# A two-layer trunk with attention: the norms' inverse roots reach all partitions by a round trip through device memory (softmax heads) and by transposes of a repeated column (the other norms)

## The chip, the cores and the metric

The kernel runs on one core of a Trainium2 chip. The metric is the device time of one execution in microseconds; for the kernel before, three runs gave 1161.12, 1161.31 and 1162.6, a median of 1161.31 us. The engines of the core are named as in the profile: PE (matrix products), DVE, ACT and POOL (elementwise work), and SP, whose queue issues most of the transfers. Each engine executes its own program in order; semaphores tie the programs together.

## The reference

The input is (1, 512, 1024) in float32: 512 tokens of 1024 features. Each of two layers normalizes x, projects it to 3072 columns, runs eight stick-breaking heads of 64 features (a sigmoid in place of a softmax) and four differential heads (two softmaxes each, subtracted), normalizes every differential head by its 128 features, projects back, and adds a squared-ReLU network of 4096. One more norm ends it. The parts that the change touches:

```python
def rmsnorm(x, g):
    xf = x.astype(jnp.float32)
    y = xf * lax.rsqrt(jnp.mean(xf * xf, axis=-1, keepdims=True) + EPS) * g.astype(jnp.float32)
...
def differential_attention(q, k, v, lam):
...
        p = jax.nn.softmax(jnp.where(allowed, s, neg), axis=-1)
        attn = p[:, :, 0] - lam * p[:, :, 1]
        return jnp.einsum('bhqk,bhkd->bhqd', attn.astype(vh.dtype), vh)
...
        h = rmsnorm(x, attn_norm[l])
        proj = jnp.einsum('bsd,de->bse', h, w_in[l])
...
        df_out = (rmsnorm(df_heads, subln_norm[l]) * (1.0 - lambda_init)).reshape(B, S, DF_WIDTH)
        mixed = jnp.concatenate([sb_out, df_out.astype(sb_out.dtype)], axis=-1)
        x = x + jnp.einsum('bse,ed->bsd', mixed, w_o[l])
        h = rmsnorm(x, mlp_norm[l])
        u = jnp.square(jax.nn.relu(jnp.einsum('bsd,df->bsf', h, w_ff1[l])))
        x = x + jnp.einsum('bsf,fd->bsd', u, w_ff2[l])
    return rmsnorm(x, final_norm)
```

Every one of these norms multiplies each token by one number, the inverse root of a mean of squares.

## The kernel before, in words

**Layout.** Activations stand with the features on the 128 partitions and the 512 tokens along the row. A norm's factor, one number for each token, is therefore needed as a row of 512 numbers that is the same on all 128 partitions. All large products are made of three matmuls (`three`, L278): every operand is split into a high and a low part, and high by high, high by low and low by high are summed (L281 to L283 by the trace). `split` (L223) makes the parts: the high one on ACT (L224), the low one on DVE (L225).

**A norm, first half: `rms_a` (L244).** PE transposes the squares in four blocks of 128 tokens (L248), so that tokens stand on partitions; DVE sums along the row (L249) and scales the mean (L251, or L253 with a floor of its own for each token); POOL raises it to the power of minus one half (L259). The result is a column: 128 partitions by 4 blocks, `rcol` for the attention norm (a) and the MLP norm (m), `rc` for a differential head (d). Then DVE splits the column into `chi` and `clo` (L260, L261), and four 128 by 128 diagonal matrices of each are made (L264, L266), on DVE for a and m, on POOL for d.

**Second half: `rms_b` (L271).** PE multiplies a matrix of ones by the two diagonals (L274, L275), which puts each token's factor into a row on every partition, and ACT copies that from PSUM (L276), to `rbc` for a and m and to a tile `rb` of its own for d.

**The attention stage of a layer.** `dense` (L710) runs the input projection block by block in a fixed order: d0, w0, d1, w1, d2, w2, d3, w3, s0, u0, s1, u1, s2, u2, s3, u3, then the output projection of the differential heads (`wo`, L691). d is a differential head's queries and keys, w its values; s and u are the same of a pair of stick-breaking heads. Projections that come before the norm's factor is known are held back and evicted when a step counter reaches RB (32 in the first layer, 31 in the second); there `rms_b` of norm a stands, with the multiplication of the rotation tables `cos_t` and `sin_t` by `rbc`. `rms_a` stands at step RA (21 and 20). Evicted d heads are rotated (`evict_d`, L442): u and v by `cos_t` and `sin_t`, then, deferred by 3.5 us of a modelled clock, sums, a split into `hl`, and twelve moves by SP's queue (`move`, L420) into the stacks `st` (high parts) and `kl` (low parts) that the score matmuls read (L477 and L478).

Beside it runs the generator `attn` (L667): scores of a unit (`s1_df`, `s1_sb`), transposes of the weights two units later (`s2`), products with the values three units later (`s3`). The loop at L744 mixes the two: every yielded step of the projection advances a modelled clock by the cost of its matmuls and gives attention a credit; attention's steps spend it, each by the cost that it yields. A unit is let in when the clock has passed a due time set at its eviction (6 us for s, 8 us for d). `defer` (L407) runs a function when the clock has passed.

When a differential head is complete, `start_norm` (L638) calls `rms_a` with the head's squares, and one unit later `finish` (L646) calls `rms_b`, lets POOL multiply the head's output `os` by `rb` (L650), and splits it into `mdh` and `mdl` (L651), which only the output projection reads. Both yield a cost of 0.43 to the clock.

**The MLP.** Groups of eight hidden blocks follow one another; norm m's `rms_a` stands at the start of the second block of the first group (L943), its `rms_b` in the third (L945); the first two blocks wait in PSUM until then.

**Order and queues.** The tile framework's scheduler orders each engine's program from the emitted one; nothing is fixed by hand. SP's queue carries the weights' raw loads, the moves and loads of tables.

Of the kernel before, what the change touches and what calls it, by code (L numbers as in the profile page):

```python
# [9 lines left out]
F32 = mybir.dt.float32  # L10
# [7 lines left out]
P = 128  # L18
S = 512
# [12 lines left out]
LAG2, LAG3, KSB = 2, 3, 7  # L32
MTB = 1
TB = 5
RST = 2
WARM = 10
RA, RB, DLY_V = (21, 20), (32, 31), 3.5
# [114 lines left out]
def trunk(ctx, tc, xT, w, w2, gains, gfin, lamv, cos, sin, out):  # L152
# [5 lines left out]

    banks = {"t": 2, "mm": 2, "s": 3, "o": 1}
# [36 lines left out]
    ones = cp.tile([P, 1], F32, tag="ones", name="ones")  # L196
    nc.vector.memset(ones, 1.0)
# [18 lines left out]
    chi = cp.tile([P, 4], F32R, tag="chi", name="chi")  # L216
    clo = cp.tile([P, 4], F32, tag="clo", name="clo")
    ones_r = cp.tile([P, 1], F32R, tag="onesr", name="ones_r")
    nc.vector.memset(ones_r.bitcast(F32), 1.0)
    fin = cp.tile([P, 24], F32, tag="fin", name="fin")  # L220
    cp.tile([P, 88], F32, tag="trail", name="trail")
# [22 lines left out]
    def rms_a(src, inv_n, col, name, eng, dgt, floor=None):  # L244
        pt = bank("t", "rs_" + name)
        if RST and eng is not nc.gpsimd or RST == 2:
            for j in range(4):
                nc.tensor.transpose(pt[:, j * P : (j + 1) * P], src[:, j * P : (j + 1) * P], ident)  # L248
            nc.vector.tensor_reduce(out=ms, in_=pt.rearrange("p (j f) -> p j f", j=4), axis=AX.X, op=ALU.add)  # L249
            if floor is None:  # L250
                nc.vector.tensor_scalar(out=ms, in0=ms, scalar1=inv_n, scalar2=EPS, op0=ALU.mult, op1=ALU.add)  # L251
            else:
                nc.vector.scalar_tensor_tensor(  # L253
                    out=ms, in0=ms, scalar=inv_n, in1=floor, op0=ALU.mult, op1=ALU.add)
        else:
            for j in range(4):
                nc.tensor.matmul(pt[:, j : j + 1], src[:, j * P : (j + 1) * P], ones, start=True, stop=True)
            nc.vector.tensor_scalar(out=ms, in0=pt[:, 0:4], scalar1=inv_n, scalar2=EPS, op0=ALU.mult, op1=ALU.add)
        nc.gpsimd.tensor_tensor(out=col, in0=ms, in1=mhalf, op=ALU.pow)  # L259
        nc.vector.tensor_copy(chi, col)  # L260
        nc.vector.tensor_sub(clo, col, chi.bitcast(F32))  # L261
        dg_hi, dg_lo = dgt("dgh" + name), dgt("dgl" + name)
        idb = ident.unsqueeze(1).to_broadcast([P, 4, P])
        eng.tensor_mul(  # L264
            dg_hi.rearrange("p (j t) -> p j t", j=4), idb, chi.bitcast(F32).unsqueeze(2).to_broadcast([P, 4, P]))
        eng.tensor_mul(  # L266
            dg_lo.rearrange("p (j t) -> p j t", j=4), idb, clo.unsqueeze(2).to_broadcast([P, 4, P]))

        return dg_hi, dg_lo

    def rms_b(bc, name, dg, tag="t"):  # L271
        dg_hi, dg_lo = dg
        pb = bank(tag, "rb_" + name)
        nc.tensor.matmul(pb, ones_r.to_broadcast([P, P]), dg_hi, start=True, stop=False)  # L274
        nc.tensor.matmul(pb, ones_r.to_broadcast([P, P]), dg_lo, start=False, stop=True)  # L275
        nc.scalar.copy(bc, pb)  # L276
# [40 lines left out]
    for l in range(L):  # L317
        with ExitStack() as actx:
# [21 lines left out]
            def tr(name):  # L340
                return a2.tile([P, S], F32R, tag="dg", name=name)

# [57 lines left out]
            dgs = {}  # L400
# [235 lines left out]
            late = []  # L636

            def start_norm():  # L638
                b, os_, sqo, rc = late[0]
                floor = a3.tile([P, 4], F32, tag="floor", name=f"floor{l}{b}")  # L640
                nc.vector.scalar_tensor_tensor(
                    out=floor, in0=tops[b], scalar=EPS, in1=tops[b], op0=ALU.mult, op1=ALU.mult)
                dgs[b] = rms_a(sqo, 1.0 / P, rc, f"d{l}{b}", nc.gpsimd, tr, floor)
                return 0.43

            def finish():  # L646
                b, os_, _, _ = late.pop(0)
                rb = tt(f"rb{l}{b}")
                rms_b(rb, f"d{l}{b}", dgs[b], "s")
                nc.gpsimd.tensor_mul(os_, os_, rb)  # L650
                split(md_hi[:, b, :], md_lo[:, b, :], os_)  # L651
                return 0.43

            def behind_scores(i, stage):
# [5 lines left out]
                if stage == 2:  # L660
                    yield finish()
# [48 lines left out]
            def dense(pts):  # L710
# [9 lines left out]
                for item in ORDER[1:]:  # L720
                    kind, b = item[0], int(item[1])
                    for which in ("qk" if kind in "ds" else "v"):
                        name = f"p{l}{kind}{b}{which}"
                        for pt in block(name, "s" if step in (16, 24, 32) else "mm"):
                            step += 1
                            if step == RA[l]:
                                dgs["a"] = rms_a(ssq, 1.0 / D, rcol, f"a{l}", nc.vector, tr)
                            if step == RB[l]:
                                rms_b(rbc, f"a{l}", dgs["a"])
# [39 lines left out]
        with ExitStack() as fctx:  # L769
# [151 lines left out]
            def diagonals():  # L921
                f = fp.tile([P, 4, S], F32R, tag="F", name=f"diag{l}")
                parts_ = iter((f[:, 0, :], f[:, 1, :]))
                return lambda name: next(parts_)

            for g in range(GROUPS):
# [13 lines left out]
                for k in range(2 * GP):  # L940
                    for n, pt in enumerate(block(f"f{l}_{g}_{k}", "any")):
                        if (g, k, n) == (0, 1, 0):
                            dg = rms_a(ssq, 1.0 / D, rcol, f"m{l}", nc.vector, diagonals())  # L943
                        if (g, k, n) == (0, 2, 4):
                            rms_b(rbc, f"m{l}", dg)  # L945
# [139 lines left out]
```

## Time and profile before

| what | value |
|---|---|
| median of three runs | 1161.31 us |
| profiled execution, its own time | 1163.8 us |
| its span | 1162.0 us |
| mean granted PE clock | 0.998 |
| POOL busy | 17% |
| ACT busy | 52% |
| bytes moved in the span | 171.67 MB |

The profile is of one execution, and its span lies inside that execution's own time. Engines are busy side by side, so shares don't add up. A wait is idle time of an engine, put down to what ended it; a matmul's record overlaps that of the next, and its cost is read from the starts. A line number is one of the kernel before; a row of the timeline gives start, duration, engine, line, operation, output from inputs, and shape. In the rows of transfers stand KB of each and the median time from issue to landing.

### The profile page before, as it was taken

The page shows a single profiled execution, that of the slowest core. Times are in us where ns is not written, and L with a number is a line of the kernel's source. Part 1 is how long each engine was busy: PE and PEld are TensorE (multiplying, and loading weights), DVE is VectorE, ACT ScalarE, POOL GpSimd, SP SyncE. Part 2 cuts the span into 40 slices and gives each one's busy share as a digit, 9 for nine tenths or more (in the row PEclk, how much of TensorE's full clock was granted, in tenths as well). Part 3 has the DMA queues.
Part 4 walks back from the last instruction along what each step waited for, and adds up shares of the span by engine and source line. Part 5 has one row for each costly group of instructions (what it writes and reads, how often), then busy time and mean ns, then how long its engine had stood idle before and what let it go on. Part 6 is the DMA issues. An engine that isn't in the chain of part 4 may idle for free.

```text
span 1162.0 us, 15297 instructions
## 1 busy us (share of the span) xinstructions
PE 1146.6 (99%) x5458; PEld 951.7 (82%) x5458; DVE 852.9 (73%) x1385; ACT 606.2 (52%) x1075; POOL 191.8 (17%) x271
## 2 busy tenths in 40 slices
PE   9999999999999999999999999999999999999996
PEld 6888888878888888888778888888888888888885
DVE  7888788777556757767888878877676577676676
ACT  6456666545645445445344566665465354453554
POOL 1011543131101001002000125332310010010021
PEclk9999999999999999999999999999999999999999
DMA  7546433146764755737526553432757557467185
GB/s 245 157 145 188 128 109 120 63 177 178 193 178 94 202 158 106 213 134 128 144 73 180 145 165 118 136 91 74 241 121 192 170 92 207 154 99 237 52 155 146
DMA packets 57291, 171.67 MB, mean 148 GB/s; under 512 B 7168, under 2 KB 8192, under 8 KB 57216
## 3 DMA queue, kind: packets, MB, share of 16 engines
q1 hardware_dynamic: 45840, 130.83, 33.9%
q0 software_dynamic: 10656, 38.80, 19.2%
q8 instruction: 43, 0.70, 0.3%
q10 hardware_dynamic: 720, 1.07, 0.2%
q14 instruction: 32, 0.26, 0.1%
HBM read 138.17 MB, written 2.10 MB: 121 GB/s over the span
## 4 chain that ended last, share of the span: by engine, by line
PE 83%; issue 5%; DMA 5%; DVE 4%; ACT 2%; POOL 1%; POOLq 0%; SPq 0%; DVEq 0%; ACTq 0%
PE f L282 9%; PE f L283 9%; PE f L281 9%; PE x L281 4%; PE x L283 4%; PE x L282 4%; PE wo L281 2%; PE wo L282 2%; DMA q<-in_w 2%; PE wo L283 2%; DMA yx<-yx 2%; DVE wlo L117 1%; PE T1s L567 1%; PE T0s L567 1%; DVE h_lo L229 1%
## 5 line engine op out<-in xcount | busy, mean ns | idle before, releaser
L282 PE MATMUL f<-h_lo,whi 128*128 128x512 f32 x512 | 199.3, 389 | 1.0 <-DVE h_lo L229 1.0
L281 PE MATMUL f<-h_hi,whi 128*128 128x512 f32 x512 | 199.7, 390 | 0.0
L116 ACT ACTIVATE whi<-raw 128x1024 fp32r<-128x1024 f32 (+1 forms) x130 | 131.9, 1019 | 129.7 <-PE f L282 40.1
L283 PE MATMUL f<-h_hi,wlo 128*128 128x512 f32 x512 | 199.3, 389 | 0.0
L116 ACT ACTIVATE whi<-q 128x512 fp32r<-128x512 f32 x224 | 128.5, 624 | 120.6 <-PE x L283 45.8
L117 DVE TENSOR_TENSOR wlo<-raw,whi 128x1024 fp32r<-128x1024 f32 (+1 forms) x130 | 153.7, 1187 | 45.1 <-ACT whi L116 44.4
L117 DVE TENSOR_TENSOR wlo<-q,whi 128x512 fp32r<-128x512 f32 x224 | 146.0, 686 | 49.2 <-ACT whi L116 49.0
L282 PEld LDWEIGHTS f<-h_lo,whi 128*128 128x128 f32 x512 | 96.1, 188 | 21.3 <-DVE h_lo L229 1.4
L283 PEld LDWEIGHTS f<-h_hi,wlo 128*128 128x128 f32 x512 | 96.1, 188 | 20.1
L281 PEld LDWEIGHTS f<-h_hi,whi 128*128 128x128 f32 x512 | 96.1, 188 | 19.7
L225 DVE TENSOR_TENSOR Al<-F,Ah 128x256 fp32r<-128x256 f32 (+2 forms) x96 | 74.4, 778 | 44.1 <-ACT Ah L224 44.1
L797 POOL DMA_DIRECT2D q<-in_w x48 | 41.9, 874 | 388.1 <-DVE wlo L117 368.2
L282 PE MATMUL x<-wlo,Ah 128*128 128x512 f32 x256 | 99.7, 390 | 0.7 <-DVE wlo L117 0.7
L281 PE MATMUL x<-whi,Ah 128*128 128x512 f32 x256 | 99.9, 390 | 0.0
L283 PE MATMUL x<-whi,Al 128*128 128x512 f32 x256 | 99.6, 389 | 0.0
L224 ACT ACTIVATE Ah<-F 128x256 fp32r<-128x256 f32 (+2 forms) x96 | 67.2, 703 | 50.4 <-DVE F L833 48.5
L824 DVE SCALAR_TENSOR_TENSOR F<-f,rbc 128x512 f32<-128x512 f32 x64 | 43.5, 687 | 64.9 <-PE f L283 57.6
L825 ACT ACTIVATE F<-F 128x512 f32<-128x512 f32 x64 | 39.7, 624 | 37.2 <-DVE F L824 37.1
L282 PEld LDWEIGHTS x<-wlo,Ah 128*128 128x128 f32 x256 | 48.1, 188 | 11.0 <-DVE wlo L117 1.1
L283 PEld LDWEIGHTS x<-whi,Al 128*128 128x128 f32 x256 | 48.0, 188 | 10.1
L281 PEld LDWEIGHTS x<-whi,Ah 128*128 128x128 f32 x256 | 48.1, 188 | 9.8
L228 ACT ACTIVATE h_hi<-x,g_all 128x512 fp32r<-128x512 f32 x32 | 22.4, 718 | 28.7 <-DVE x L704 17.5
(1055 smaller groups left out, 2556.8 us busy)
## 6 DMA issues: line engine op xcount, KB each, us to landing
raw<-in_w SPq DMA_DIRECT2D x126, 512.0 KB, 4.1
q<-in_w SPq DMA_DIRECT2D x64, 512.0 KB, 4.3
q<-in_w POOLq DMA_DIRECT2D x64, 512.0 KB, 5.4
yx<-yx POOLq DMA_DIRECT2D x6, 512.0 KB, 6.7
x<-in_xT SPq DMA_DIRECT2D x8, 256.0 KB, 4.5
raw<-in_w SPq DMA_DIRECT2D x8, 128.0 KB, 4.4
yx<-y POOLq DMA_DIRECT2D x2, 512.0 KB, 5.7
y<-y POOLq DMA_DIRECT2D x2, 512.0 KB, 8.7
```

Of the source, the lines that this page charges most:

```text
L116: h = nc.scalar.activation(hi[:, a:b], raw[:, a:b], AF.Copy)
L117: self.last = h, nc.vector.tensor_tensor(out=lo[:, a:b], in0=raw[:, a:b], in1=hi[:, a:b].bitcast(F32), op=ALU.subtract)
L224: nc.scalar.activation(hi, src, AF.Copy)
L225: nc.vector.tensor_tensor(out=lo, in0=src, in1=hi.bitcast(F32), op=ALU.subtract)
L228: a = nc.scalar.activation(h_hi[:, c, :], x[:, c, :], AF.Copy, scale=g)
L281: nc.tensor.matmul(pt, ah, bh, start=first, stop=False)
L282: nc.tensor.matmul(pt, ah, bl, start=False, stop=False)
L283: nc.tensor.matmul(pt, al, bh, start=False, stop=last)
L567: nc.tensor.transpose(pt[:, off : off + P], u["w"][qi][:, kb * P : (kb + 1) * P], ident)
L797: nc.gpsimd.dma_start(t, quad(g, q, c), accum_op=ALU.add)
L824: nc.vector.scalar_tensor_tensor(out=t, in0=pt, scalar=0.0, in1=rbc, op0=ALU.max, op1=ALU.mult)
L825: nc.scalar.activation(t, t, AF.Square)
```

## The change

The two diagonals, the matrix of ones and the column's high and low parts go. For norms a and m, `rms_b` now transposes each of the four columns of `rcol`, repeated 128 times along the row by its access pattern, which gives the row on all partitions; it stands ROW = 5 steps behind `rms_a`, and the evictions with the rotation tables stand at steps 29 and 28. For a differential head, SP's queue writes the column `rc` (128 by 4, 2 KB) to a tile in device memory, and `finish` reads it back, the same 2 KB for each of the 128 partitions (256 KB), into `rb`, in a buffer of its own. POOL's multiplication reads it in permuted order, and with the split it is deferred by 5 us of the modelled clock. `finish` costs that clock nothing. Score tiles have 8 buffers in place of 7; a pad in SBUF grows from 88 to 120 numbers; a branch that was not taken goes.

```diff
--- before.py
+++ after.py
@@ -29,12 +29,12 @@
 NEG = -1.0e30
 MMC = 0.000422
 ORDER = ("d0", "w0", "d1", "w1", "d2", "w2", "d3", "w3", "s0", "u0", "s1", "u1", "s2", "u2", "s3", "u3")
-LAG2, LAG3, KSB = 2, 3, 7
+LAG2, LAG3, KSB = 2, 3, 8
 MTB = 1
 TB = 5
-RST = 2
+ROW, DLY_N = 5, 5.0
 WARM = 10
-RA, RB, DLY_V = (21, 20), (32, 31), 3.5
+RA, RB, DLY_V = (21, 20), (29, 28), 3.5
 MAN = ()
 _CTX = {}
 DLY_R, DLY_D, DLY_S = 3.5, 8.0, 6.0
@@ -155,6 +155,8 @@
     wraw = ctx.enter_context(tc.tile_pool(name="wraw", bufs=3))
     wspl = ctx.enter_context(tc.tile_pool(name="wspl", bufs=2))
     ps = ctx.enter_context(tc.tile_pool(name="ps", bufs=2, space=PSUM))
+
+    far = ctx.enter_context(tc.tile_pool(name="far", bufs=2, space=bass.MemoryType.DRAM))
 
     banks = {"t": 2, "mm": 2, "s": 3, "o": 1}
     turn = [0]
@@ -193,8 +195,6 @@
     W.load(3)
 
     make_identity(nc, ident)
-    ones = cp.tile([P, 1], F32, tag="ones", name="ones")
-    nc.vector.memset(ones, 1.0)
     mhalf = cp.tile([P, 4], F32, tag="mhalf", name="mhalf")
     nc.vector.memset(mhalf, -0.5)
     nc.gpsimd.memset(edge[:, 0:384], 0.0)
@@ -213,12 +213,8 @@
     gsub = cp.tile([P, L], F32, tag="gsub", name="gsub")
     rcol = cp.tile([P, 4], F32, tag="rcol", name="rcol")
     ms = cp.tile([P, 4], F32, tag="ms", name="ms")
-    chi = cp.tile([P, 4], F32R, tag="chi", name="chi")
-    clo = cp.tile([P, 4], F32, tag="clo", name="clo")
-    ones_r = cp.tile([P, 1], F32R, tag="onesr", name="ones_r")
-    nc.vector.memset(ones_r.bitcast(F32), 1.0)
     fin = cp.tile([P, 24], F32, tag="fin", name="fin")
-    cp.tile([P, 88], F32, tag="trail", name="trail")
+    cp.tile([P, 120], F32, tag="trail", name="trail")
 
     def split(hi, lo, src):
         nc.scalar.activation(hi, src, AF.Copy)
@@ -241,39 +237,23 @@
         tc.add_manual_dep(a.ins, b.ins.name, mybir.DependencyInfo(
             mybir.DependencyClass.NoSync, mybir.DependencyReason.DATA), reason="order")
 
-    def rms_a(src, inv_n, col, name, eng, dgt, floor=None):
+    def rms_a(src, inv_n, col, name, floor=None):
         pt = bank("t", "rs_" + name)
-        if RST and eng is not nc.gpsimd or RST == 2:
-            for j in range(4):
-                nc.tensor.transpose(pt[:, j * P : (j + 1) * P], src[:, j * P : (j + 1) * P], ident)
-            nc.vector.tensor_reduce(out=ms, in_=pt.rearrange("p (j f) -> p j f", j=4), axis=AX.X, op=ALU.add)
-            if floor is None:
-                nc.vector.tensor_scalar(out=ms, in0=ms, scalar1=inv_n, scalar2=EPS, op0=ALU.mult, op1=ALU.add)
-            else:
-                nc.vector.scalar_tensor_tensor(
-                    out=ms, in0=ms, scalar=inv_n, in1=floor, op0=ALU.mult, op1=ALU.add)
+        for j in range(4):
+            nc.tensor.transpose(pt[:, j * P : (j + 1) * P], src[:, j * P : (j + 1) * P], ident)
+        nc.vector.tensor_reduce(out=ms, in_=pt.rearrange("p (j f) -> p j f", j=4), axis=AX.X, op=ALU.add)
+        if floor is None:
+            nc.vector.tensor_scalar(out=ms, in0=ms, scalar1=inv_n, scalar2=EPS, op0=ALU.mult, op1=ALU.add)
         else:
-            for j in range(4):
-                nc.tensor.matmul(pt[:, j : j + 1], src[:, j * P : (j + 1) * P], ones, start=True, stop=True)
-            nc.vector.tensor_scalar(out=ms, in0=pt[:, 0:4], scalar1=inv_n, scalar2=EPS, op0=ALU.mult, op1=ALU.add)
+            nc.vector.scalar_tensor_tensor(
+                out=ms, in0=ms, scalar=inv_n, in1=floor, op0=ALU.mult, op1=ALU.add)
         nc.gpsimd.tensor_tensor(out=col, in0=ms, in1=mhalf, op=ALU.pow)
-        nc.vector.tensor_copy(chi, col)
-        nc.vector.tensor_sub(clo, col, chi.bitcast(F32))
-        dg_hi, dg_lo = dgt("dgh" + name), dgt("dgl" + name)
-        idb = ident.unsqueeze(1).to_broadcast([P, 4, P])
-        eng.tensor_mul(
-            dg_hi.rearrange("p (j t) -> p j t", j=4), idb, chi.bitcast(F32).unsqueeze(2).to_broadcast([P, 4, P]))
-        eng.tensor_mul(
-            dg_lo.rearrange("p (j t) -> p j t", j=4), idb, clo.unsqueeze(2).to_broadcast([P, 4, P]))
-
-        return dg_hi, dg_lo
-
-    def rms_b(bc, name, dg, tag="t"):
-        dg_hi, dg_lo = dg
-        pb = bank(tag, "rb_" + name)
-        nc.tensor.matmul(pb, ones_r.to_broadcast([P, P]), dg_hi, start=True, stop=False)
-        nc.tensor.matmul(pb, ones_r.to_broadcast([P, P]), dg_lo, start=False, stop=True)
-        nc.scalar.copy(bc, pb)
+
+    def rms_b(bc, name, col):
+        pt = bank("t", "rb_" + name)
+        for j in range(4):
+            nc.tensor.transpose(pt[:, j * P : (j + 1) * P], col[:, j : j + 1].to_broadcast([P, P]), ident)
+        nc.scalar.copy(bc, pt)
 
     def three(pt, a, b, first, last):
         ah, al = a
@@ -336,9 +316,6 @@
 
             def tt(name):
                 return a2.tile([P, S], F32, tag="t", name=name, bufs=TB)
-
-            def tr(name):
-                return a2.tile([P, S], F32R, tag="dg", name=name)
 
             def parts(name):
                 return a2.tile([P, 2, 2, S], F32R, tag="hl", name=name)
@@ -397,7 +374,6 @@
                 defer(DLY_V, rest)
 
             stacks = {}
-            dgs = {}
             heads = {}
             tops = {}
             ends = {}
@@ -633,23 +609,31 @@
             def ok(key):
                 return ready.get(key, 1e9) <= clock[0]
 
-            late = []
+            late, rows = [], {}
 
             def start_norm():
                 b, os_, sqo, rc = late[0]
                 floor = a3.tile([P, 4], F32, tag="floor", name=f"floor{l}{b}")
                 nc.vector.scalar_tensor_tensor(
                     out=floor, in0=tops[b], scalar=EPS, in1=tops[b], op0=ALU.mult, op1=ALU.mult)
-                dgs[b] = rms_a(sqo, 1.0 / P, rc, f"d{l}{b}", nc.gpsimd, tr, floor)
+                rms_a(sqo, 1.0 / P, rc, f"d{l}{b}", floor)
+                rows[b] = far.tile([P, 4], F32, tag="row", name=f"row{l}{b}")
+                nc.sync.dma_start(rows[b], rc)
                 return 0.43
 
             def finish():
                 b, os_, _, _ = late.pop(0)
-                rb = tt(f"rb{l}{b}")
-                rms_b(rb, f"d{l}{b}", dgs[b], "s")
-                nc.gpsimd.tensor_mul(os_, os_, rb)
-                split(md_hi[:, b, :], md_lo[:, b, :], os_)
-                return 0.43
+                rb = a2.tile([P, S], F32, tag="rb", name=f"rb{l}{b}", bufs=1)
+                nc.sync.dma_start(rb, rows[b].rearrange("t j -> (t j)").partition_broadcast(P))
+
+                def rest():
+                    nc.gpsimd.tensor_mul(
+                        os_.rearrange("p (j t) -> p j t", j=4), os_.rearrange("p (j t) -> p j t", j=4),
+                        rb.rearrange("p (t j) -> p j t", j=4))
+                    split(md_hi[:, b, :], md_lo[:, b, :], os_)
+
+                defer(DLY_N, rest)
+                return 0
 
             def behind_scores(i, stage):
                 n = len(units)
@@ -658,7 +642,7 @@
                 if 0 <= i - LAG2 < n:
                     yield from s2(units[i - LAG2])
                 if stage == 2:
-                    yield finish()
+                    finish()
                 if 0 <= i - LAG3 < n:
                     while not ok(("v" + units[i - LAG3]["kind"], units[i - LAG3]["b"])):
                         yield 0
@@ -724,9 +708,10 @@
                         for pt in block(name, "s" if step in (16, 24, 32) else "mm"):
                             step += 1
                             if step == RA[l]:
-                                dgs["a"] = rms_a(ssq, 1.0 / D, rcol, f"a{l}", nc.vector, tr)
+                                rms_a(ssq, 1.0 / D, rcol, f"a{l}")
+                            if step == RA[l] + ROW:
+                                rms_b(rbc, f"a{l}", rcol)
                             if step == RB[l]:
-                                rms_b(rbc, f"a{l}", dgs["a"])
                                 nc.vector.tensor_mul(cos_t, cos_t, rbc)
                                 nc.vector.tensor_mul(sin_t, sin_t, rbc)
                             yield 3 * 0.216
@@ -918,11 +903,6 @@
                 n = turn[0] = turn[0] + 1
                 return spare[0][:, 2 * (n % 4) : 2 * (n % 4) + 2, :].rearrange("p a t -> p (a t)")
 
-            def diagonals():
-                f = fp.tile([P, 4, S], F32R, tag="F", name=f"diag{l}")
-                parts_ = iter((f[:, 0, :], f[:, 1, :]))
-                return lambda name: next(parts_)
-
             for g in range(GROUPS):
                 forms = {}
                 end = g == GROUPS - 1
@@ -940,9 +920,9 @@
                 for k in range(2 * GP):
                     for n, pt in enumerate(block(f"f{l}_{g}_{k}", "any")):
                         if (g, k, n) == (0, 1, 0):
-                            dg = rms_a(ssq, 1.0 / D, rcol, f"m{l}", nc.vector, diagonals())
-                        if (g, k, n) == (0, 2, 4):
-                            rms_b(rbc, f"m{l}", dg)
+                            rms_a(ssq, 1.0 / D, rcol, f"m{l}")
+                        if (g, k, n) == (0, 1, ROW):
+                            rms_b(rbc, f"m{l}", rcol)
                     waiting.append((pt, k))
                     if g == 0 and k < 2:
                         continue
```

## The prediction

> **What bounds the kernel now.** I read the page first: what share each engine is busy, and whether TensorE's clock holds.
>
> ```profile
> span 1162.0 us, 15297 instructions
> ...
> PE 1146.6 (99%) x5458; PEld 951.7 (82%) x5458; DVE 852.9 (73%) x1385; ACT 606.2 (52%) x1075; POOL 191.8 (17%) x271
> ...
> PEclk9999999999999999999999999999999999999999
> ```
>
> PE is busy 99% of the span at an undisturbed clock, so the time is the number of matmuls by their pace, plus the gaps. DVE (73%) and POOL (17%) have room: what the change takes from them (the columns' hi/lo parts, the diagonals) I cost at nothing, under the cover of PE's matmuls. Without that cover it could only be a gain. The next view is what PE waited for:
>
> ```profile
> PE f L282 <- DVE h_lo L229: 1.0, 1, 1.0
> ...
> PE S1d L477 <- DMA st1d3q<-hl1d3k: 0.7, 1, 0.7
> ```
>
> Single waits of 1 us and less. One is of interest: the second layer's first score matmul of head d3 waits for a transfer, so there is no slack there for the change to eat. Now the price of PE's instructions, from the timeline (start, duration):
>
> ```profile
> 79.33 0.60 PE L248 MATMUL rs_d<-edge,sqo 128*128 128x128 f32 x4
> 79.69 0.48 PE L281 MATMUL p0d3k<-h_hi,whi 128*128 128x512 f32 x1
> 80.00 0.39 PE L282 MATMUL p0d3k<-h_lo,whi 128*128 128x512 f32 x1
> 80.23 0.39 PE L283 MATMUL p0d3k<-h_hi,wlo 128*128 128x512 f32 x1
> ```
>
> Durations overlap, so starts count. A 512-wide matmul costs 0.23 us (80.00 to 80.23). Four transposes with the matmul behind them cost 0.67 (79.33 to 80.00), the transposes alone 0.44.
>
> **The change, part by part.**
>
> *1. Matmuls removed.* Eight softmax heads lose two 512-wide matmuls each: 16 x 0.23 = **-3.7 us**, on the bound engine. The norms a and m lose two and get four transposes, four times over: 0.46 against 0.44, nothing.
>
> *2. Norm a's transposes come too soon.* Transposes of the column wait only for POOL's pow, and the order of the built kernel puts them seven matmuls behind the sums' transposes (rs_a), where before the diagonals' matmuls stood some twenty behind. PE's arrival is the start of the eighth matmul behind rs_a today, the column is there at the pow's end:
>
> ```profile
> 24.93 2.05 POOL L259 TENSOR_TENSOR rcol<-ms,mhalf 128x4 f32<-128x4 f32 x1 [22.63 <-DVE nlam L313]
> 25.37 0.39 PE L283 MATMUL p0d1q<-h_hi,mdl 128*128 128x512 f32 x1
> ...
> 28.78 0.39 PE L283 MATMUL p0d1q<-h_hi,mdl 128*128 128x512 f32 x1
> 29.14 0.47 PE L274 MATMUL rb_a<-dgha,ones_r 128*128 128x512 f32 x1
> ...
> 29.98 0.39 PE L281 MATMUL p0d1k<-h_hi,whi 128*128 128x512 f32 x1
> ...
> 599.56 1.03 POOL L259 TENSOR_TENSOR rcol<-ms,mhalf 128x4 f32<-128x4 f32 x1 [12.39 <-DVE ms L251]
> 599.64 0.39 PE L281 MATMUL p1d1q<-h_hi,mdh 128*128 128x512 f32 x1
> ...
> 601.46 0.39 PE L283 MATMUL p1d1q<-h_hi,mdl 128*128 128x512 f32 x1
> 602.58 0.40 PE L281 MATMUL p1d1q<-h_hi,mdh 128*128 128x512 f32 x1
> ```
>
> First layer: ready at 24.93 + 2.05 = 26.98, arrival 25.37, wait 1.6, and 0.1 to refill (79.69 to 80.00 is 0.31, not 0.23). What goes: 28.78 to 29.98 is 1.20 for three matmuls' 0.69, so a wait of 0.5. Net **+1.2**. Second: ready 600.59, arrival 599.64, wait 0.95 and refill; 601.46 to 602.58 is 1.12, 0.43 of it a wait that goes. Net **+0.65**. Behind the waiting transposes stands PE's whole program, so every wait is paid in full. The bounds: nothing, if the chain in front of the pow turns quicker by the wait (DVE has less to do), and 1.7 and 1.05, if the old waits come back elsewhere.
>
> *3. Norm m likewise.* Its transposes stand fifteen matmuls behind rs_m:
>
> ```profile
> 256.76 1.02 POOL L259 TENSOR_TENSOR rcol<-ms,mhalf 128x4 f32<-128x4 f32 x1 [5.64 <-DVE ms L251]
> 256.85 0.39 PE L281 MATMUL f<-h_hi,whi 128*128 128x512 f32 x1
> ...
> 830.45 1.02 POOL L259 TENSOR_TENSOR rcol<-ms,mhalf 128x4 f32<-128x4 f32 x1 [5.50 <-DVE ms L251]
> 830.81 0.39 PE L281 MATMUL f<-h_hi,whi 128*128 128x512 f32 x1
> ```
>
> Waits of 257.78 - 256.85 = 0.93 and 831.47 - 830.81 = 0.66, each with 0.1 of refill; the pair that goes did not wait. Net **+1.05 and +0.75**, bounds nothing and the same again.
>
> *4. The softmax heads' two transfers, and who waits.* The column goes out (2 KB) and comes back spread (256 KB), both on SP's queue; then POOL multiplies, and ACT makes mdh. In the built order ACT's mdh of head 0 stands directly ahead of hl of d3's rotated queries, in both layers; before it came long after. ACT waits in order: behind mdh stand that hl, an Exp, and the weight splits, and behind hl the twelve moves without which PE can't start d3's scores.
>
> ```profile
> 81.55 1.02 POOL L259 TENSOR_TENSOR rc<-ms,mhalf 128x4 f32<-128x4 f32 x1 [54.57 <-DVE ms L253]
> 88.70 0.63 ACT L224 ACTIVATE hl0d3k<-u0d3q 128x512 fp32r<-128x512 f32 x1 [3.20 <-DVE u0d3q L453]
> 89.36 1.19 SPq L420 DMA_DIRECT2D st0d3k<-hl0d3k  x2
> 96.65 0.47 PE L477 MATMUL S0d<-st0d3k,st0d3q 128*128 128x256 f32 x2
> 98.28 1.34 POOL L650 TENSOR_TENSOR os<-os,rb 128x512 f32<-128x512 f32 x1 [12.79 <-ACT rb L276]
> 655.08 1.01 POOL L259 TENSOR_TENSOR rc<-ms,mhalf 128x4 f32<-128x4 f32 x1 [54.49 <-DVE ms L253]
> 663.87 0.61 ACT L224 ACTIVATE hl1d3k<-u1d3q 128x512 fp32r<-128x512 f32 x1
> 671.87 0.47 PE L477 MATMUL S1d<-st1d3k,st1d3q 128*128 128x256 f32 x2 [0.74 <-DMA st1d3q<-hl1d3k]
> ```
>
> The trace has no such pair of transfers. The nearest by kind are these (KB, median from issue to landing), the writes to device memory and the loads spread over 128 partitions:
>
> ```profile
> out_xT<-y ACTq DMA_DIRECT2D x2, 256.0 KB, 2.1
> ...
> g_all<-in_gains ACTq DMA_DIRECT2D x1, 21.0 KB, 3.0
> ...
> cos_t<-in_gfin SPq DMA_DIRECT2D x1, 256.0 KB, 3.4
> sin_t<-in_gfin SPq DMA_DIRECT2D x1, 256.0 KB, 4.2
> ```
>
> I take 2.1 for the write (it is the only write, bounds 2.1 and 3.0) and 3.9 for the spread (bounds 3.4 and 4.2). First layer: pow's end 82.57 + 2.1 + 3.9 + POOL 1.34 + mdh 0.63 + hl 0.63 + moves 7.3 (89.36 to 96.65, where PE came with next to no slack) = 98.5, with the hops about 98.7. PE arrives at 96.65 less the two matmuls that go from this stretch, 96.2. Wait **+2.5**, bounds 2.0 and 3.7 by the rows' ends. Second: 656.09 + 15.9 + hops = 672.2, 0.35 behind the 671.87 of before, and the two matmuls that term 1 counts as saved in this stretch, 0.45, are lost in the same wait: **+0.8**, bounds 0.3 and 2.0. For heads 1 to 3 the same transfers stand in SP's queue ahead of s0's moves and between raw loads, with several us until PE needs what is behind them: nothing, with part of the upper end if not.
>
> The Trainium skill ("DMA: Bandwidth & Descriptors", Anatomy of one DMA) speaks against chaining two small transfers: each has a fixed cost of about 2.0 us, most of it the confirmation of the write at the target, plus bytes over 436 KB per us. That would be an estimate of 2.0 + 2.6 = 4.6 us in place of my 6.0, so a sum smaller by 1.4 or so in the first layer. The landings of cos_t and sin_t are longer than its 2.6, and the measured rows decide.
>
> *5. Scores come sooner.* The change lets finish() cost nothing on the clock that paces attention between the projections, so stick-breaking units are let in sooner. The closest is head s3:
>
> ```profile
> 180.76 0.39 PE L283 MATMUL p0s3k<-h_hi,wlo 128*128 128x512 f32 x1
> 184.37 1.43 SPq L420 DMA_DIRECT2D kl0s3k<-hl0s3q  x2
> 190.90 0.28 PE L478 MATMUL S0s<-kl0s3k,st0s3q 128*128 128x256 f32 x1
> ...
> kl0s3k<-hl0s3q SPq DMA_DIRECT2D x2, 256.0 KB, 5.2
> ...
> kl1s3k<-hl1s3q SPq DMA_DIRECT2D x2, 256.0 KB, 4.1
> ```
>
> Today 10.1 us lie between the last projection matmul and the first that needs kl; in the built order it is 24 wide matmuls, five of 256 columns and seven transposes, about 6.8. The moves start 3.6 behind the matmul: with 4.1 to landing they are there after 7.7, with 5.2 after 8.8. I take 4.1 for both layers, **+0.85 each**, bounds nothing and 2.0; it is nearest because less of the raw loads' traffic stands before moves that come earlier.
>
> *6. The rest.* A score buffer more, a larger pad, evictions three steps earlier: no instructions; at most a wait less. Nothing.
>
> **The sum**: -3.7 + 1.2 + 0.65 + 1.05 + 0.75 + 2.5 + 0.8 + 1.7 = **+5.0 us**. The profiled execution took 1163.8 (span 1162.0 and 1.8 around it), so 1168.8 under the profiler. The median of the runs shown is 1161.31, 2.5 lower: **1166.3**.
>
> **The rivals.**
>
> *A, faster: the latencies are shorter than I read.* All eight waits are latencies (pow, landing, moves), not work; the profiled run is 2.5 us longer than the median, so they may be shorter without profiling. Place: PE in front of rb_a, rb_m and the scores of d3 and s3. They sum to 8.7; below 3.7, each shorter by 0.6, the kernel is faster, and at 0.9 less for each about 1.6 is left: -3.7 + 1.6, **1159**; with none, 1157.6. Against it: 2.5 us is 0.2% of the span, which spread evenly is next to nothing of a 3 us chain.
>
> *B, a tie: only the transposes wait.* If the transfers land in 3.5 together, or ACT's order leaves hl its place, terms 4 and 5 go, and the matmuls saved are what the transposes lose: -3.7 + 3.7, **1161.3**. That also is the case in which the change does not reach its aim because POOL's pow stays the source of the wait. For it: the first layer came to d3 with its moves just landed, so small errors decide. Against: two transfers in 3.5 is less than any two rows here.
>
> *C, much slower: SP's queue piles up.* If the spread takes as long as a move under load (5.2), or head-of-line waits reach s0 to s2, each of d3's two waits grows by 1.3 to 2 and other heads add theirs: +9 to +12, **1170 to 1173**. Against it: those heads have several us.
>
> The Trainium skill ("TensorE: Matmul & The Clock Gate", Why this matters for your kernels) warns that a PE gap beyond about 3 us halves the clock for a while. The longest wait forecast is 2.5, and before shows no such gap, so it can't be checked here; it belongs to C.
>
> **How the numbers follow.** Forecast 0.54 (1163.7 to 1169.5 by the terms' bounds), A 0.12, B 0.21, C 0.13. A measurement can tell about 0.2%, 2.3 us: faster is below 1159.0, slower above 1163.6. B, with a tenth of the edges, is within: 0.22; A is 0.12; forecast and C are slower: 0.66. The range 1159.5 to 1171 leaves out most of A and half of C, less than 0.2.
>
> **What would show it.** In the changed profile: 16 wide matmuls fewer; PE waiting on POOL's rcol before the transposes, 1.6, 0.95, 0.9, 0.7; S0d of d3 waiting some 2.5 on its moves, with ACT's hl behind an mdh that waits on POOL; row landing 2.1, rb 3.9; S0s and S1s of s3 waiting up to 1 on kl. The prediction is wrong if PE's waits there are under half of these, or if other waits over 1 us appear.

## The result and the profile after

The changed kernel takes 1178.41 us (median of four runs, 1176.21 to 1178.61) against 1161.65 of before: the ratio is 1.0139, with a 95% interval of 1.0127 to 1.0152. The forecast was slower by 5 us; it is slower by 16.8. The profiled execution took 1178.44, with a span of 1176.7, so 14.7 more span than before; the profiled execution of before, 1163.8, lies 2 us above its median, which is why the spans differ by less than the medians. The 14.7 have to be found in the trace.

The page of the changed kernel, the lines that answer to those shown of before:

```profile
span 1176.7 us, 15260 instructions
...
PE 1146.6 (97%) x5450; PEld 950.6 (81%) x5450; DVE 835.2 (71%) x1351; ACT 603.5 (51%) x1067; POOL 185.1 (16%) x255
```

DVE and POOL do less, as the change intends, and PE has dropped from 99% to 97%: the new time is waiting. What PE waited for (total, times, longest; O is a unit's product with the values, T the transposes of its weights):

```profile
PE rb_a L255 <- POOL rcol L250: 2.3, 2, 1.5
PE S1s L454 <- DMA kl1s0k<-hl1s0q: 2.2, 1, 2.2
PE S0s L454 <- DMA kl0s0k<-hl0s0q: 2.1, 1, 2.1
PE O0s L571 <- DVE mt L586: 1.7, 1, 1.7
...
PE vT1w L363 <- DVE tv1w L358: 1.3, 1, 1.3
PE rb_m L255 <- POOL rcol L250: 1.1, 2, 0.6
PE S1d L453 <- DMA st1d3q<-hl1d3k: 1.1, 1, 1.1
PE S0d L453 <- DMA st0d3q<-hl0d3k: 1.1, 1, 1.1
...
PE T0s L543 <- DVE fl0s L221: 0.9, 1, 0.9
PE S1s L454 <- DMA kl1s3k<-hl1s3q: 0.8, 1, 0.8
```

Most of these waits are new (before had 0.6 at vT1w and 0.7 at S1d), and they come in three families: waits on transfers (kl of s0 and s3, the stacks of d3), waits on the column that POOL makes, and waits on DVE, which is not short of time (71% busy). This view leaves out the refill behind a wait, so for the account I took the starts of PE's matmuls: each gap between two starts, less that matmul's pace. The terms, first and second layer, old waits that went already taken off:

| term | forecast | measured from the starts |
|---|---|---|
| 16 matmuls fewer | -3.7 | -3.7 |
| norm a's transposes | +1.2, +0.65 | +1.27, +0.68 |
| norm m's transposes | +1.05, +0.75 | +0.72, +0.72 |
| d3's scores, with the transposes of w3's values (vT w) ahead of them | +2.5, +0.8 | +2.40, +1.05 |
| s3's scores | +0.85, +0.85 | +0.95, +1.00 |
| s0's scores | 0 | +2.24, +2.39 and 1.65 of slow matmuls behind the second |
| O and T of stick-breaking units, under the last softmax head's norm (d3) | 0 | +2.94, +1.46 |
| the wait f on h_lo of the first layer | 0 | -1.18 |

They sum to +14.6, the span's 14.7. The four terms that the forecast priced came to 8.8 where it had 8.7. Two that it put at nothing, 6.3 and 4.4, hold the miss.

**The chain at d3 in the first layer**, on the timeline, from the pow to the scores:

```profile
81.90 1.25 POOL L250 TENSOR_TENSOR rc<-ms,mhalf 128x4 f32<-128x4 f32 x1 [55.14 <-DVE ms L248]
...
83.17 0.33 SPq L621 DMA_DIRECT2D row<-rc  x1
...
84.59 0.33 SPq L627 DMA_DIRECT2D rb<-row  x1
...
89.37 1.54 POOL L630 TENSOR_TENSOR os<-os,rb 128x512 f32<-128x512 f32 x1 [6.22 <-DMA rb<-row]
...
90.94 0.63 ACT L220 ACTIVATE mdh<-os 128x512 fp32r<-128x512 f32 x1 [4.67 <-POOL os L630]
91.48 0.62 ACT L220 ACTIVATE hl0d3k<-u0d3q 128x512 fp32r<-128x512 f32 x1
...
92.12 1.19 SPq L396 DMA_DIRECT2D st0d3k<-hl0d3k  x2
...
99.37 0.47 PE L453 MATMUL S0d<-st0d3k,st0d3q 128*128 128x256 f32 x2 [1.09 <-DMA st0d3q<-hl0d3k]
```

This is the forecast's step 4 as it was written, for head d0's norm: ACT idles 4.67 us in front of mdh, and hl, which nothing else kept waiting, comes only behind it. The row and its spread cost 1.4 and 4.6 to landing, 6.0 together.

**The same at the norm of the last softmax head, d3**, which the forecast did not see. In the window from 143 us:

```profile
147.97 0.32 SPq L627 DMA_DIRECT2D rb<-row  x1
...
154.13 1.53 POOL L630 TENSOR_TENSOR os<-os,rb 128x512 f32<-128x512 f32 x1 [5.93 <-DMA rb<-row]
...
155.70 0.63 ACT L220 ACTIVATE mdh<-os 128x512 fp32r<-128x512 f32 x1 [5.99 <-POOL os L630]
...
156.37 0.69 DVE L221 TENSOR_TENSOR mdl<-os,mdh 128x512 fp32r<-128x512 f32 x1 [6.07 <-ACT mdh L220]
...
159.20 0.38 PE L571 MATMUL O0s<-zh,vs 128*128 128x256 f32 x1 [1.70 <-DVE mt L586]
```

Three engines stand idle for six microseconds behind one transfer, and then have the work of six microseconds to make up. PE runs out of what they prepare, at O0s and a little later at T0s.

**s0's scores.** SP's queue of the changed kernel on the timeline:

```profile
108.91 0.33 SPq L621 DMA_DIRECT2D row<-rc  x1
109.34 1.18 SPq L396 DMA_DIRECT2D st0s0k<-hl0s0q  x2
110.61 0.56 SPq L99 DMA_DIRECT2D raw<-in_w  x1
111.26 1.59 SPq L396 DMA_DIRECT2D kl0s0k<-hl0s0q  x2
112.95 0.78 SPq L627 DMA_DIRECT2D rb<-row  x1
```

and, from the view of transfers, the landing:

```profile
kl0s0k<-hl0s0q SPq DMA_DIRECT2D x2, 256.0 KB, 6.4
```

Before, kl's two moves stood directly behind those of st, and the weight load behind them:

```profile
106.02 1.18 SPq L420 DMA_DIRECT2D st0s0k<-hl0s0q  x2
107.50 1.34 SPq L420 DMA_DIRECT2D kl0s0k<-hl0s0q  x2
108.89 7.13 SPq L99 DMA_DIRECT2D raw<-in_w  x2
```

The first use of kl, without a wait, was

```profile
114.08 0.28 PE L478 MATMUL S0s<-kl0s0k,st0s0q 128*128 128x256 f32 x1
```

and, from the view of transfers, the landing:

```profile
kl0s0k<-hl0s0q SPq DMA_DIRECT2D x2, 256.0 KB, 4.0
```

A 512 KB load has slipped in front of kl, whose landing grows from 4.0 to 6.4 us. The row that SP waits for (108.91) is not what delays: st0s0k needs the hl that ACT writes from 108.53 on in any case. And in the order of the matmuls 8.5 us of work, where it was 10.7 by the starts, lie between s0's last projection matmul and the first use of kl. Before, the first of kl's two moves had landed (107.50, and 3.7 to landing) 2.9 us ahead of that use. The matmuls take 2.1 us of these, and kl, counted from s0's last projection matmul, lands 2.9 later.

### The profile page after: what moved, and what is told of

Read it like the earlier page. It is cut to its first block, busy times and chain, and to the rows that moved or that the text cites. A ratio compares the mean times of both kernels' runs of the same rounds, so it can differ in the third digit from the quotient of the medians.

```text
span 1176.7 us, 15260 instructions
## 1 busy us (share of the span) xinstructions
PE 1146.6 (97%) x5450; PEld 950.6 (81%) x5450; DVE 835.2 (71%) x1351; ACT 603.5 (51%) x1067; POOL 185.1 (16%) x255
## 4 chain that ended last, share of the span: by engine, by line
PE 71%; DMA 9%; issue 8%; DVE 6%; ACT 3%; POOL 3%; SPq 0%; POOLq 0%; DVEq 0%; ACTq 0%
PE f L261 8%; PE f L263 8%; PE f L262 8%; PE x L261 4%; PE x L262 4%; PE x L263 4%; PE wo L261 2%; PE wo L262 2%; PE wo L263 2%; DMA q<-in_w 2%; DMA yx<-yx 2%; DVE wlo L117 2%; DMA rb<-row 1%; DMA x<-in_xT 1%; ACT whi L116 1%
## 5 line engine op out<-in xcount | busy, mean ns | idle before, releaser
L262 PEld LDWEIGHTS x<-wlo,Ah 128*128 128x128 f32 x256 | 48.1, 188 | 10.7 <-DVE wlo L117 0.9
L474 POOL TENSOR_TENSOR sig1s<-sig1s,C1s 128x128 f32<-128x128 f32 (+3 forms) x32 | 28.6, 893 | 52.6 <-DVE C1s L471 41.1
```

The source lines that it names most:

```text
L262: nc.tensor.matmul(pt, ah, bl, start=False, stop=False)
L474: nc.gpsimd.tensor_mul(sig[:, 0:wd], sig[:, 0:wd], C[:, 1 : wd + 1])
```

## The experiments

Given are medians, each with that of the kernel before measured on the same chip. The theory before each: PE pays every wait in full, and the waits come from (1) transposes placed ahead of their column, (2) ACT held by mdh behind a transfer, (3) scores let in too soon, with s0's kl behind a load.

**e1, norms a and m alone.** On the kernel before:

```diff
+    def rms_t(bc, name, col):
+        pt = bank("t", "rb_" + name)
+        for j in range(4):
+            nc.tensor.transpose(pt[:, j * P : (j + 1) * P], col[:, j : j + 1].to_broadcast([P, P]), ident)
+        nc.scalar.copy(bc, pt)
...
-RA, RB, DLY_V = (21, 20), (32, 31), 3.5
+RA, RB, DLY_V = (21, 20), (29, 28), 3.5
...
+                            if step == RA[l] + 5:
+                                rms_t(rbc, f"a{l}", rcol)
...
-                        if (g, k, n) == (0, 2, 4):
-                            rms_b(rbc, f"m{l}", dg)
+                        if (g, k, n) == (0, 1, 5):
+                            rms_t(rbc, f"m{l}", rcol)
```

> The kernel before with only norms a and m spread by transposes (5 steps behind the sums, evictions at 29 and 28); the softmax heads keep their diagonals. Theory (every wait of PE is paid in full, and the changed kernel's 14.6 us are its listed waits less 3.7 of matmuls): waits of 1.7, 1.0, 0.7, 0.7 before the transposes, 0.75 of old waits gone, so +3.4 us, up to +4.5 if d3's scores, which now come 0.7 us sooner, catch up with their moves: 1165 to 1166. Rival (PE gives such waits back later, because everything else runs ahead meanwhile): within 1 us of before.

Measured: 1165.24 against 1161.92, ratio 1.0027 (1.0018 to 1.0037), +3.3 us. Its waits:

```profile
PE rb_a L283 <- POOL rcol L259: 2.5, 2, 1.7
...
PE rb_m L283 <- POOL rcol L259: 1.3, 2, 0.8
```

The waits are there and are not given back. This half of the change costs what the forecast said.

**e2, the softmax heads alone.** On the kernel before, with KSB 8 and the new start_norm and finish; norms a and m keep their diagonals (norm a's in buffers of the score tiles, for space).

```diff
+                rows[b] = far.tile([P, 4], F32, tag="row", name=f"row{l}{b}")
+                nc.sync.dma_start(rows[b], rc)
...
-                rms_b(rb, f"d{l}{b}", dgs[b], "s")
+                nc.sync.dma_start(rb, rows[b].rearrange("t j -> (t j)").partition_broadcast(P))
...
-                    yield finish()
+                    finish()
```

> The kernel before with only the softmax heads' two transfers, and the new pacing; norms a and m keep their diagonals. Theory: the changed kernel's 14.6 us less the 3.4 of norms a and m, about +11: 1172 to 1174, with waits at d3, s0, s2 and s3. Rival (the two parts hurt each other through the earlier evictions): clearly under +8.

Measured: 1169.89 against 1161.92, ratio 1.0068 (1.0049 to 1.0087), +8.0: a miss, on the edge to the rival. The parts don't add up to the whole, 3.3 and 8.0 against 16.8. The trace says where: here no weight load stands between s0's st and kl in SP's queue, and

```profile
PE S0s L482 <- DMA kl0s0k<-hl0s0q: 0.5, 1, 0.5
```

stands in place of 2.1, and 0.4 in place of 2.2 in the second layer, with no slow matmuls behind it. By the starts that is 5.0 of the 5.5 us missing. The other waits (vT w, O0s, T0s, s3) are there as in the changed kernel, within 0.8 us of it. The rival's reason, the earlier evictions, is not shown: the load stands ahead of kl in e8 too, which has none. What moves it was not tried.

**e3, pacing restored.** On the changed kernel:

```diff
                 defer(DLY_N, rest)
-                return 0
+                return 0.43
...
-                    finish()
+                    yield finish()
```

> The changed kernel with finish() charging 0.43 to the pacing clock again, as before; the transfers, their queue and the transposes stay. The order of its matmuls puts 10.4 us (not 8.5) between s0's last projection matmul and its first use of kl, and 10.0 (not 6.8) for s3. Theory (scores let in too soon): s0's waits fall from 2.2 and 2.4 to about 0.4, s3's 0.95 and 1.0 go, the slow matmuls after 701 go, so about 6 to 7 us faster than the changed kernel, near 1172. Rival (the weight load ahead of s0's kl in SP's queue is the cause, the pacing not): s0's waits stay above 1.5, and only the 2 us of s3 go, near 1176.5.

Measured: 1165.94 against 1161.92, ratio 1.0035 (1.0023 to 1.0047): 12.5 less than the changed kernel's 1178.41, twice what was expected. All waits of s0 and s3 are gone, with the slow matmuls, and so are those of O0s and T0s: the expectation had not tied the 4.4 us of O and T to the pacing. What is left in the list, beside waits of before, are the transposes', d3's and one new wait of 0.9:

```profile
PE rb_a L255 <- POOL rcol L250: 2.4, 2, 1.5
PE vT1w L363 <- DVE tv1w L358: 1.5, 1, 1.5
...
PE S0d L453 <- DMA st0d3q<-hl0d3k: 1.1, 1, 1.1
PE rb_m L255 <- POOL rcol L250: 1.1, 2, 0.6
...
PE rs_d L243 <- ACT sqo L592: 0.9, 1, 0.9
```

The new one is of the same family: ACT's sqo stands behind an mdh that ACT idled 5.93 us for. So finish() at no cost on the clock let the stick-breaking units in too close to what they need: one charge to the pacing clock, more than two thirds of the loss.

**e4, the split of every softmax head late.** On the changed kernel, with DLY_N 10:

```diff
-                    nc.gpsimd.tensor_mul(
+                    a = nc.gpsimd.tensor_mul(
...
-                    split(md_hi[:, b, :], md_lo[:, b, :], os_)
+                    if "mul" in ends:
+                        behind(a, ends["mul"])
+                    split(md_hi[:, b, :], md_lo[:, b, :], os_, recent[0])
```

`recent[0]` is the newest split on ACT, `ends["mul"]` POOL's newest stick-breaking multiplication; `behind` orders one instruction after another on its engine.

> The changed kernel with the split of a finished softmax head ordered on ACT behind the newest other split (and POOL's multiplication behind the newest stick-breaking one), deferred by 10 us of the modelled clock in place of 5: mdh then stands after d3's hl and not before it. The transfers stay as they are. Theory (ACT stands behind a transfer): waits at vT w of 1.15 and 1.5, at d3's scores of 1.25 and 1.25, at O0s and T0s of 2.9 and 1.5 go, of which 1.7 was there before the change: 7 to 8 us faster than the changed kernel, near 1171. Rival (the moves themselves are late because the row and its spread crowd SP's queue): d3's waits stay, under 3 us gained.

Measured: 1193.15 against 1161.92, ratio 1.0262 (1.0233 to 1.0292), 15 slower than the changed kernel. Theory and rival both missed the total. In the first layer d3's waits went, as the theory said, and in the second they fell to 1.09 and 1.04 by the starts, near the 0.77 and 0.91 of before. But a later mdh keeps `os`, and os has one buffer, shared with the next head's output and with `mt` of the stick-breaking heads:

```profile
PE O0d L266 <- ACT os L598: 2.7, 1, 2.7
...
PE O0s L576 <- ACT os L598: 2.5, 1, 2.5
```

ACT can't copy the next head out of PSUM until mdh and mdl have read the last, and PE can't start the next product. The split has a latest place too.

**e5, transfers without a reader.** On the changed kernel:

```diff
-                        rb.rearrange("p (t j) -> p j t", j=4))
+                        rbc.rearrange("p (t j) -> p j t", j=4))
```

> The changed kernel with POOL's multiplication reading rbc in place of rb (so the softmax heads get the wrong roots): both transfers are still issued and landed, and nothing waits for them. Theory (ACT, and DVE behind it, stand behind the landing): the waits at vT w (1.15, 1.5), d3's scores (1.25, 1.25), O0s and T0s (2.9, 1.5) go, of which 1.7 was there before the change, and s0's and s3's stay: about 7.5 us faster than the changed kernel, near 1171. Rival (the transfers slow the moves beside them in SP's queue): d3's waits stay at 1 or more each, under 3 us gained.

Measured: 1169.14 against 1162.18, ratio 1.0060 (1.0039 to 1.0080), 9.3 less than the changed kernel. The waits at O0s, O1s, T0s and T1s and d3's in the first layer are gone, those of the second are 1.33 and 0.79 by the starts (before: 0.77 and 0.91), and s0 (2.5 and 2.1) and s3 wait as they did. The transfers still land, the spread in 4.6 to 8.0 us (4.2 to 6.2 in the changed kernel): what costs most is that readers wait for them in order. Two limits: with nothing to wait for, mdh also moved ahead in ACT's order (81.25, where ACT did not idle), and d3's moves, now issued while the spread and a load are under way, land later: kl in 3.9 in the first layer and 5.1 in the second (medians), 2.7 and 2.8 in the changed kernel. Whether that makes the 0.44 that the second layer waits beyond before, or the two matmuls saved ahead of it, is open.

**e6, pacing and late transposes.** e3 with the transposes of a and m where the diagonals' matmuls stood:

```diff
-RA, RB, DLY_V = (21, 20), (29, 28), 3.5
+RA, RB, DLY_V = (21, 20), (32, 31), 3.5
...
-                            if step == RA[l] + ROW:
+                            if step == RB[l]:
...
-                        if (g, k, n) == (0, 1, ROW):
+                        if (g, k, n) == (0, 2, 4):
```

> Pacing restored as in the run before (1165.9), and the transposes of norms a and m where the diagonals' matmuls stood (steps 32 and 31; third hidden block). Theory: the waits of 1.7, 1.0, 0.7, 0.7 go, about 4 us: 1162, with d3's two waits left. Rival (a wait taken away comes back at the next late transfer): 1164 or more.

Measured: 1160.80 against 1162.18, ratio 0.9983 (0.9975 to 0.9992), as the theory said and not the rival. No wait for rcol is left in the list. What is left is at d3 and in front of it:

```profile
PE vT1w L363 <- DVE tv1w L358: 1.7, 1, 1.7
PE vT0w L363 <- DVE tv0w L358: 1.6, 1, 1.6
...
PE S0d L454 <- DMA kl0d3k<-hl0d3k: 0.8, 1, 0.8
```

**e7, the first head's split behind d3's hl.** e6 with

```diff
-                    split(md_hi[:, b, :], md_lo[:, b, :], os_)
+                    split(md_hi[:, b, :], md_lo[:, b, :], os_, recent[0] if b == 0 else None)
 
-                defer(DLY_N, rest)
+                defer(DLY_0 if b == 0 else DLY_N, rest)
```

> As the run with pacing and late transposes, and in each layer the first head's mdh ordered behind d3's hl on ACT (that head's deferral 8 us in place of 5; the other heads stay as they were). Theory: d3's waits go (1.25 and 1.28 in the first layer, 1.67 and 1.18 less the 1.7 of before in the second), about 3.5 us: 1158.5, and with it the 16 matmuls saved are seen, 3 us faster than before. Rival (ACT's next instruction then waits for mdh as long): within 1 us of the run without this edit.

Measured: 1157.37 against 1162.18, ratio 0.9949 (0.9937 to 0.9961), 3.4 less than e6. This version beats both kernels. From its page:

```profile
span 1154.7 us, 15258 instructions
...
PE 1142.0 (99%) x5450; PEld 949.2 (82%) x5450; DVE 836.4 (72%) x1351; ACT 601.2 (52%) x1067; POOL 176.2 (15%) x255
```

PE is back at 99%, with the matmuls saved. d3's scores wait no more in either layer, and of the waits in front of them only that of the second layer is left, 0.8, which the kernel before had too (0.6). A longer deferral alone would not have done it: e6 built with 8, 10 or 14 in place of 5 has the same order in every engine's program. It took the ordering on ACT.

**e8, no transfers at all.** e6 with the softmax heads' roots spread by four transposes of a repeated `rc`:

```diff
-                nc.sync.dma_start(rb, rows[b].rearrange("t j -> (t j)").partition_broadcast(P))
+                rms_b(rb, f"d{l}{b}", rc, "s")
```

> No transfers at all: the softmax heads' roots too are spread by four transposes of a repeated column, at the place of the diagonals' matmuls; late transposes for a and m; pacing as before. Theory: 0.44 us of transposes in place of 0.46 of matmuls for every norm, no wait added, so within 1.5 us of before (1161.9), and the gain of the run with the late mdh needs the transfers. Rival (the diagonals cost more than PE's two matmuls, through DVE and POOL): 2 us or more faster than before.

Measured: 1159.85 against 1162.18, ratio 0.9973 (0.9962 to 0.9985): 2.3 less than before, the rival's result. By PE's starts, before's waits at vT w and d3 of the second layer (1.7) and at rb_a (0.75) are gone. So is one of 0.87 at x near the end, which comes and goes between the runs; nothing else differs by more than 0.4. It seems that the diagonals carried waits with them, but which of the removed instructions caused them was not tried. The transfers with the split well placed gain 2.5 more.

**e9, s0's kl ahead of the load.** On the changed kernel; a weight load or spread issued while s0's moves are the newest is ordered behind them:

```diff
+            d = self.nc.sync.dma_start(t, self.dram[self.loaded])
+            if self.moved is not None:
+                self.behind(d, self.moved)
...
+                if W.moved is not None:
+                    behind(d, W.moved)
```

> The changed kernel with one thing moved: in SP's queue s0's kl moves stand ahead of the weight load (and of the second head's spread behind it) that stood ahead of them; PE's order is the same, matmul by matmul, so the scores come as soon as in the changed kernel. Theory (of s0's lateness, 2 us come from the pacing and 3 from the load: kl issued 0.65 sooner and landing in 4.0 as before, not 6.4): s0's waits of 2.2 and 2.4 go, and with the second the slow matmuls behind it, so about 5 to 6 us faster than the changed kernel, near 1173. Rival (the pacing alone makes s0 wait, and the load is an accident): over 1.5 us of wait stays at each, under 2 us gained.

Measured: 1173.61 against 1162.95, ratio 1.0090 (1.0073 to 1.0107), 4.8 less than the changed kernel, just under what the theory said. SP's queue:

```profile
109.30 1.18 SPq L401 DMA_DIRECT2D st0s0k<-hl0s0q  x2
110.69 1.49 SPq L401 DMA_DIRECT2D kl0s0k<-hl0s0q  x2
```

and, from the view of transfers, the landing:

```profile
kl0s0k<-hl0s0q SPq DMA_DIRECT2D x2, 256.0 KB, 4.2
```

No wait of s0 is left in either layer. With e3, where the load still stands ahead of kl, it says that s0's wait took both: the scores 2 us sooner and kl 3 us later. Either one undone ends it; e1 and e8, with the pacing of before and the load ahead of kl (landing in 6.0), don't wait there either. The wait f on h_lo came back, 1.0 in each layer (before: in the first).

## Why the prediction was wrong

The direction was right, and so was the mechanism of every term that was priced. The forecast failed where it put two terms at nothing: the heads 1 to 3 in step 4, and every stick-breaking head but s3 in step 5. +5 was forecast, +16.8 measured; waits over 1 us at other places were the forecast's own sign of being wrong.

- **Matmuls removed, -3.7**: right by the count and the pace. e7, 4.8 below before, agrees; no run removes them alone.
- **Transposes too soon, +1.85 and +1.8**: right, 1.95 and 1.44, alone in e1 and gone in e6.
- **d3 behind mdh, +2.5 and +0.8**: right, 2.40 and 1.05, and e5 and e7 show the cause: ACT's place behind the landing, more than the traffic. That the two transfers took the 6.0 forecast was luck: 2.1 and 3.9 were forecast, 1.4 and 4.6 came. PE took part of the wait ahead of the scores, at vT w, since DVE, too, stood behind hl (3.57 us idle until ACT's hl) with tv0w queued behind it.
- **s3's scores, +1.7**: right, 1.95.
- **"For heads 1 to 3 ... nothing"**: here it failed. The same mechanism, ACT and DVE behind a spread, was at work at the last head, d3: 2.94 and 1.46 us, 4.4 in all. The forecast asked only what stood behind these transfers in SP's queue, not what stood behind their readers on ACT, DVE and POOL. It showed only because step 5's pacing put that mdh among units that PE needs soon: e3 removes PE's wait with the pacing alone, though ACT still idles 3.4 us there, where it was 6.0.
- **Step 5 priced only the "closest" head.** s3 had least time left in PE's order, but s0 lost its time twice, 2.1 us of matmuls and 2.9 of kl's landing, because the load had changed places with kl. That was 4.6 in the two layers and 1.65 of slow matmuls. The forecast gave these heads "several us" until PE needs their moves; before had 2.9 us there, and the exchange alone used them up.
- Rival C (SP's queue piles up, heads s0 to s2 add their own waits, 1170 to 1173) named the place and had 0.13; it was still short by 5. Rivals A and B fell: the waits were as long as read, and the two transfers took 6.0 together. Nor did profiling lengthen the run: the changed kernel's profiled execution, 1178.44, is at its median, so the 2.5 us that A leaned on belonged to one execution of before. The Trainium skill ("DMA: Bandwidth & Descriptors", Anatomy of one DMA), from which the prediction has its estimate of 4.6, gives the figure for transfers that GpSimd issues; these are SP's, and took 6.0.

## What to carry to other kernels

A transfer's latency is paid where its reader stands in an in-order engine: for each new reader, list what is queued behind it, for every instance of the loop and not only the first. When a modelled clock paces work, a step that becomes free on that clock lets all that follows in sooner, so measure the shortest distances between a producer and its user again. An instruction that waits has an earliest useful place and a latest, set by the buffer that it frees: e7's place for one head gained 3.4 us; e4's places for all, with POOL's multiplication put back as well, cost 15.

## What the runs showed of the hardware

A wait of PE of some 2.2 us can be followed by a cost beyond itself. Behind s0's wait in the second layer, the timeline of the changed kernel shows starts 0.43 apart where 0.23 is usual (702.26 to 702.69):

```profile
698.97 0.39 PE L454 MATMUL S1s<-kl1s0k,st1s0q 128*128 128x256 f32 x1 [2.23 <-DMA kl1s0k<-hl1s0q]
...
702.26 0.63 PE L261 MATMUL p1s1q<-h_hi,whi 128*128 128x512 f32 x1
702.69 0.63 PE L262 MATMUL p1s1q<-h_lo,whi 128*128 128x512 f32 x1
```

Its windows give the busy time and the instructions of PE, weight loads, DVE, ACT and POOL, then the granted clock, the transfers' share and GB/s:

```profile
699.00:701.00 2.00, 2.00 (x9) 1.70 (x10) 0.61 (x2) 1.59 (x4) 0.65 (x1) 0.71 0.07 24
701.00:703.00 2.00, 2.00 (x7) 1.71 (x6) 2.00 (x2) 0.72 (x3) 2.00 (x2) 0.50 0.00 0
703.00:705.00 2.00, 2.00 (x13) 1.68 (x13) 1.65 (x4) 0.74 (x2) 1.13 (x3) 0.94 0.42 115
```

By the windows' means the granted clock is at 0.50 for about 3.4 us, from 0.9 us after the wait on, and the slow starts add 1.65 us. The wait of the first layer, 2.08, had no such phase; in e5 the wait of 2.50 in the first layer had one and that of 2.08 in the second none. Of e4's eight longest gaps, 2.7 to 3.1 us by the starts, five had one, which began up to 1.4 us behind the gap's end and once 0.2 ahead of it. The Trainium skill ("TensorE: Matmul & The Clock Gate", Why this matters for your kernels) puts the limit at gaps above about 3 us; here a wait of 2.23 was enough, and not each longer one was.

The write of the 2 KB row, in pieces of 16 bytes, landed in 1.4 us five times of eight, below every landing of before (2.0 and more), and in 2.2 the other three. s0's moves of 256 KB landed in 6.4 behind a load of 512 KB (the changed kernel, first layer) and in 4.2 ahead of it (e9), as medians of two.
